# A run of extra matmuls behind the last product of a decoder trunk, into two PSUM banks that nobody reads

## The chip, the core and the metric

The kernel runs on one core of one Trainium2 chip. The metric is the device time of one execution in microseconds (us); lower is better. A difference counts as one when it is over 2%.

## The reference, cut to what matters

A small decoder trunk over 256 tokens of width 2048: a recurrent block (RG-LRU), an MLP, a dilated attention block and a second MLP, each with an RMS norm ahead of it and a residual add behind it, and a final norm.

```python
def _mlp(h, w1, w2):
    u = jnp.einsum('bsd,df->bsf', h, w1)          # 2048 -> 8192
    u = jnp.square(jax.nn.relu(u))
    return jnp.einsum('bsf,fd->bsd', u, w2)       # 8192 -> 2048

def reference(x, ...):
    for i in range(DEPTH):                        # DEPTH = 2
        h = _rmsnorm(x, mix_norm[i])
        x = x + (_rglru_block(h, ...) if i % 2 == 0 else _dilated_attention_block(h, ...))
        x = x + _mlp(_rmsnorm(x, mlp_norm[i]), mlp_w1[i], mlp_w2[i])
    return _rmsnorm(x, final_norm)
```

The change adds nothing to the result: what it computes is not in the reference.

## The kernel before

All products are made on TensorE (PE) in a rounded 32-bit float type (float32r). Each operand is split into a high part and a low part, and a product is three matmuls into the same accumulator: high by high, high by low, low by high. The still operand of a matmul (128 by 128) is loaded into the array by a weight load of its own, the moving operand is streamed through it in 128, 256 or 512 columns, and the result is added up in one of eight PSUM banks of 512 columns. Weight tiles of 128 by 2048 come by DMA into `raw`; ScalarE (ACT) makes their high part `whi`, VectorE (DVE) the low part `wlo`.

`xT` are four tiles of normed, turned activations. Each has four blocks of 512 elements, and a block holds, for 128 rows of the model's width, two token halves `t` (even and odd tokens), each as a high and a low part `u`, each of 128 tokens `q`, so its order in memory is (t u q). Where a block moves through the array it is read "in turn": one element of the even half, then one of the odd half, 256 elements apart. `moving`, `in_turn` and `by_turn` are the access patterns for this; `moving(x, 0)` is the high part of all 256 tokens, `moving(x, 1)` the low part. `mm` (line 201) issues every matmul.

The kernel opens with ten warm-up matmuls, then works through a list of items, each some 48 matmuls on one or two weight units: the recurrent block, the first MLP, attention, the second MLP. The order on PE is the order in which the Python code issues the matmuls; each engine works through its own list in order, and semaphores hold it where data or a buffer is not ready. PE is fed from the pool `psum`: `acc` (four banks), `tr` (two) and `g` (two). `g` serves the first products of the MLPs; its last use before the change is some 45 us ahead of PE's last matmul.

The last part of the program is `final_items`: the last chunk of 512 model columns is made for the first 128 tokens, normed and sent out while the second 128 tokens are computed in two banks, one half each (`first_halves`, which issues each matmul as two of 256 columns, alternating between the two banks, and `last_half`). Behind the last matmul a short chain on DVE and ACT adds the residual, forms the norm and scales the rows, and the rows go out by DMA. At the end SyncE (SP) waits for everything that is under way, and the engines meet at a barrier.

```python
    def moving(x, u):
        return x.rearrange("p (t u q) -> p u q t", t=2, u=2)[:, u]
    ...
                        mm(bank[:, s], aT(k)[:, x + 128:x + 256],
                           in_turn(w[:, j * 512:(j + 1) * 512], s.start, 256), starts, False)
```

Of the kernel before, what the change touches and what calls it, by code (L numbers as in the profile page):

```python
# [10 lines left out]
F32 = mybir.dt.float32  # L11
# [65 lines left out]
def trunk(ctx: ExitStack, tc: tile.TileContext, a: dict, out: bass.AP):  # L77
    nc = tc.nc
    P = 128
# [3 lines left out]
    psum = ctx.enter_context(tc.tile_pool(name="psum", bufs=1, space=bass.MemoryType.PSUM))  # L83
# [116 lines left out]
    def mm(o, l, r, start, stop):  # L200
        nc.tensor.matmul(o, l, r, start=start, stop=stop, skip_group_check=True)  # L201
# [6 lines left out]
    def pcol(name, j):  # L208
        at = PC[name][0] + j
        return par[:, at:at + 1]  # L210
# [3 lines left out]
    state = {}  # L214
# [5 lines left out]
    def new_xT(n):  # L220
        t = perm.tile([P, 4, 512], F32R, name=f"xT{n}")
        state["xT", n] = t
        return t
# [39 lines left out]
    def moving(x, u):  # L263
        return x.rearrange("p (t u q) -> p u q t", t=2, u=2)[:, u]
# [769 lines left out]
        state["gB"] = gB  # L1034


    first = [None] * FIRST
    lru.open("rec")
    plan_rec()
# [26 lines left out]
    for n in range(NCH):  # L1066
        x = new_xg(n)
        t = new_xT(n)
# [6 lines left out]
        for i in range(max(len(cols), len(loads))):  # L1075
# [9 lines left out]
        order = ("x0", "w0", "x1", "x2", "x3", "w1", "w2", "w3") if n == 0 else (  # L1085
            "x0", "x1", "x2", "w0", "x3", "w1", "w2", "w3")
        for what in order:
            k = int(what[1])
# [4 lines left out]
            g = pcol("mix0", 4 * n + k)  # L1093
# [39 lines left out]
    for at in range(len(items) - 1, -1, -1):  # L1133
        u = items[at][0]
        least[at] = least[at + 1] if u is None else min(u, least[at + 1])
    least = least[1:]
    for at, (u, fn, kind) in enumerate(items):
# [15 lines left out]
            sums_of_tokens()  # L1153
        now[0] += 1
    assert not later, sorted(later)
    lru.close()


# [83 lines left out]
```

## Time and profile before

| | |
|---|---|
| time, median of 2 runs | 2021.47 us (2021.29 to 2021.66) |
| the profiled execution's own time | 2022.14 us |
| its span, first to last instruction | 2020.4 us |
| mean granted TensorE clock | 0.999 |
| PE busy | 2006.2 us, 99% of the span, 13761 matmuls |
| PE weight loads | 13761 |
| DVE, ACT, POOL busy | 1724.6, 1293.7, 88.4 us |

The span leaves out 1.74 us of the execution's time, and this execution was 0.67 us above the median. In the rows below PE is the matmul engine, PEld its weight loads; a row of the timeline has the start in us, the busy time in us, the engine, the line, the operation, what it writes and reads, the shape and how many instructions are merged in it. The busy time of a matmul is from its start to the modelled end of its pipeline, so the time that a matmul takes in a stream is read from the distance of two starts.

### The profile page before, as it was taken

To read this page: it belongs to the slowest core of one execution; us is meant where nothing else is said; L and a number is where in the kernel's file an instruction comes from. 1 tells how busy PE (TensorE), PEld (TensorE's weight loads), DVE (VectorE), ACT (ScalarE), POOL (GpSimd) and SP (SyncE) were. 2 spreads that over 40 slices of the span, in tenths; PEclk is the share of its full clock that TensorE was granted. 3 is DMA by queue.
4 is the path that set the end of the run, shared out by engine and by line. 5 is a ranking of instruction groups with operands and counts; after the bars stand their busy time and mean duration, and the time that the engine had idled before them with its cause. 6 is when DMAs were issued, how large, how long until landed. Compare 5 with 4: busy or idle time off the path is not lost.

```text
span 2020.4 us, 32932 instructions
## 1 busy us (share of the span) xinstructions
PE 2006.2 (99%) x13761; PEld 1876.2 (93%) x13761; DVE 1724.6 (85%) x1903; ACT 1293.7 (64%) x1420; POOL 88.4 (4%) x83
## 2 busy tenths in 40 slices
PE   9999999999999999999999999999999999999998
PEld 9999988999999999999889989889999999999997
DVE  7999865699999999998658959857999999999985
ACT  7878775566566666665657657656666666666664
POOL 0111110000000000000000000000000000000001
PEclk9999999999999999999999999999999999999999
DMA  8555565688787788777554555456787877887774
GB/s 310 204 195 201 183 229 190 246 252 250 258 284 264 230 292 270 248 238 255 197 214 175 186 188 179 176 193 245 250 250 264 283 265 228 297 270 248 233 260 153
DMA packets 68917, 472.54 MB, mean 234 GB/s; under 512 B 7584, under 2 KB 7712, under 8 KB 13472
## 3 DMA queue, kind: packets, MB, share of 16 engines
q1 hardware_dynamic: 60416, 411.18, 54.2%
q0 software_dynamic: 8064, 58.72, 14.6%
q8 instruction: 108, 1.77, 0.3%
q10 hardware_dynamic: 288, 0.52, 0.1%
q14 instruction: 41, 0.34, 0.0%
HBM read 409.58 MB, written 2.10 MB: 204 GB/s over the span
## 4 chain that ended last, share of the span: by engine, by line
PE 91%; DVE 6%; ACT 2%; issue 1%; DMA 0%; SPq 0%; DVEq 0%; ACTq 0%
PE acc L201 44%; PE g L201 29%; PE tr L201 17%; DVE wlo L136 3%; ACT whi L132 1%; DVE qT L682 1%; PE tr L242 0%; DVE xc L686 0%; DVE c L437 0%; PE tr L853 0%; DVE sT L625 0%; DVE uu L592 0%; DVE aT L601 0%; DMA par<-in_par 0%; DVE sw L612 0%
## 5 line engine op out<-in xcount | busy, mean ns | idle before, releaser
L132 ACT ACTIVATE whi<-raw 128x2048 fp32r<-128x2048 f32 (+1 forms) x309 | 568.9, 1845 | 317.1 <-PE acc L201 163.1
L136 DVE TENSOR_TENSOR wlo<-raw,whi 128x2048 fp32r<-128x2048 f32 (+1 forms) x309 | 678.1, 2197 | 96.7 <-ACT whi L132 96.3
L201 PE MATMUL g<-xT,whi 128*128 128x256 f32 x3649 | 617.1, 275 | 0.0
L201 PEld LDWEIGHTS g<-xT,whi 128*128 128x128 f32 x3649 | 553.9, 192 | 0.0
L201 PE MATMUL g<-xT,wlo 128*128 128x256 f32 x1824 | 503.0, 276 | 0.6 <-DVE wlo L136 0.4
L201 PE MATMUL acc<-xT,whi 128*128 128x256 f32 (+1 forms) x2212 | 456.3, 301 | 0.3 <-ACT whi L132 0.3
L201 PE MATMUL acc<-xT,wlo 128*128 128x256 f32 x1360 | 374.1, 275 | 0.6 <-DVE wlo L136 0.6
L201 PEld LDWEIGHTS acc<-xT,whi 128*128 128x128 f32 x2212 | 356.3, 192 | 14.4 <-ACT whi L132 1.2
L201 PEld LDWEIGHTS g<-xT,wlo 128*128 128x128 f32 x1824 | 350.1, 192 | 2.2 <-DVE wlo L136 1.1
L201 PE MATMUL acc<-whi,aT 128*128 128x512 f32 (+1 forms) x1086 | 322.9, 374 | 0.0
L136 DVE TENSOR_TENSOR wlo<-q,whi 128x2048 fp32r<-128x2048 f32 x112 | 255.8, 2284 | 23.5 <-ACT whi L132 23.2
L132 ACT ACTIVATE whi<-q 128x2048 fp32r<-128x2048 f32 x112 | 214.4, 1915 | 79.3 <-PE g L201 53.3
L201 PEld LDWEIGHTS acc<-xT,wlo 128*128 128x128 f32 x1360 | 261.9, 193 | 1.4 <-DVE wlo L136 1.3
L201 PEld LDWEIGHTS acc<-whi,aT 128*128 128x128 f32 x1086 | 204.0, 189 | 27.6
L201 PE MATMUL tr<-whi,sT 128*128 128x512 f32 (+1 forms) x728 | 212.8, 364 | 0.9
L201 PE MATMUL acc<-wlo,aT 128*128 128x512 f32 (+1 forms) x536 | 200.8, 376 | 0.0
L132 ACT ACTIVATE whi<-qT 128x2048 fp32r<-128x2048 f32 x56 | 107.6, 1922 | 127.5 <-PE g L201 93.0
L201 PEld LDWEIGHTS tr<-whi,sT 128*128 128x128 f32 x728 | 137.7, 189 | 24.1 <-issue 6.1
L201 PE MATMUL tr<-whi,aT 128*128 128x512 f32 (+1 forms) x462 | 140.3, 373 | 0.0
L136 DVE TENSOR_TENSOR wlo<-qT,whi 128x2048 fp32r<-128x2048 f32 x56 | 127.9, 2284 | 1.3 <-ACT whi L132 1.3
L201 PE MATMUL tr<-wlo,sT 128*128 128x512 f32 x336 | 127.3, 379 | 0.0
L201 PEld LDWEIGHTS acc<-wlo,aT 128*128 128x128 f32 x536 | 101.1, 189 | 13.2
(170 smaller groups left out, 2147.5 us busy)
## 6 DMA issues: line engine op xcount, KB each, us to landing
raw<-in_w SPq DMA_DIRECT2D x172, 1024.0 KB, 6.9
q<-in_w SPq DMA_DIRECT2D x84, 1024.0 KB, 8.0
raw<-in_w_in SPq DMA_DIRECT2D x35, 1024.0 KB, 4.8
raw<-in_w_qk SPq DMA_DIRECT2D x32, 1024.0 KB, 4.8
q<-q POOLq DMA_DIRECT2D x28, 1024.0 KB, 12.2
q<-qT POOLq DMA_DIRECT2D x28, 1024.0 KB, 7.5
raw<-in_w_out SPq DMA_DIRECT2D x20, 1024.0 KB, 4.8
raw<-in_w_v SPq DMA_DIRECT2D x16, 1024.0 KB, 4.8
```

The costliest lines, as they stand in the source:

```text
L132: nc.scalar.activation(split[i][0][:, s], r, AF.Copy)
L136: nc.vector.tensor_sub(split[i][1][:, s], r, split[i][0][:, s].bitcast(F32))
L201: nc.tensor.matmul(o, l, r, start=start, stop=stop, skip_group_check=True)
L682: nc.vector.tensor_add(q[to], q[a], q[b])
```

## The change

A function `probes` is called once, behind the last item and ahead of the closing of the pools. It takes the two banks of the pool's name `g`, opens each with one matmul of 512 columns, and then issues 23 runs of 24 matmuls each that go on adding to these banks: 2 + 552 = 554 matmuls. Fifteen runs (360 matmuls) have 256 columns, eight runs (192) have 512. Nothing reads the banks. The runs differ in where the results go (one half of a bank, its two halves in turn, two banks in turn, or changing every three), in the still operand (a new block of `xT1` or `xT2` each time, each used twice, or always the same), and in the order in which the moving block of `xT0` is read.

```diff
+    def probes():
+        banks = [psum.tile([P, 512], F32, name="g", bufs=2) for _ in range(2)]
+        for b in banks:
+            mm(b, state["xT", 1][:, 0, 0:128], state["xT", 0][:, 0, :], True, True)
+        flat = [state["xT", n][:, :, :].rearrange("p k s -> p (k s)") for n in range(4)]
+        def weights(n, k):
+            return flat[1 + n][:, 128 * k:128 * k + 128]
+        def tokens(k, u):
+            return moving(state["xT", 0][:, k, :], u)
+        def run(to, still, read, count=24):
+            for j in range(count):
+                mm(to(j), weights(*still(j)), read(j), False, j == count - 1)
+        one = lambda j: banks[0][:, 0:256]
+        halves_of = lambda j: banks[0][:, 256 * (j % 2):256 * (j % 2) + 256]
+        both_of = lambda j: banks[j % 2][:, 0:256]
+        far = lambda j: banks[j % 2][:, 256 * (j % 2):256 * (j % 2) + 256]
+        thirds = lambda j: banks[0][:, 0:256] if j % 6 < 3 else banks[1][:, 0:256]
+        new = lambda j: (j % 2, j % 16)
+        real = lambda j: ((0, 0, 1)[j % 3], j // 3 % 16)
+        same = lambda j: (0, 3)
+        pair = lambda j: (0, j // 2 % 16)
+        hl = lambda j: tokens(j // 3 % 4, (0, 1, 0)[j % 3])
+        hi = lambda j: tokens(j % 4, 0)
+        fixed = lambda j: tokens(0, 0)
+        for to in (one, halves_of, both_of, far, thirds):
+            run(to, real, hl)
+        for to in (one, halves_of, both_of):
+            run(to, new, hi)
+        for to in (one, halves_of, both_of):
+            run(to, same, hi)
+        for to in (one, halves_of):
+            run(to, pair, hi)
+        run(one, new, fixed)
+        run(halves_of, same, fixed)
+        whole = lambda j: banks[0]
+        turns = lambda j: banks[j % 2]
+        for order in ("u q t", "q t u", "q u t", "u t q"):
+            run(whole, new, lambda j: state["xT", 0][:, j % 4, :].rearrange(f"p (t u q) -> p {order}", t=2, u=2))
+        run(turns, new, lambda j: state["xT", 0][:, j % 4, :].rearrange("p (t u q) -> p u q t", t=2, u=2))
+        run(whole, same, lambda j: state["xT", 0][:, j % 4, :].rearrange("p (t q) -> p q t", t=2))
+        run(whole, new, lambda j: state["xT", 0][:, j % 4, :].rearrange("p (t q) -> p q t", t=2))
+        run(turns, new, lambda j: state["xT", 0][:, j % 4, :].rearrange("p (t q) -> p q t", t=2))
...
     assert not later, sorted(later)
+    probes()
     lru.close()
```

On PE, at the end of its list, the difference begins like this (a minus stands before rows of the kernel before, a plus before rows of the changed one; `x2` merges two rows that read alike):

```order
 L201 MATMUL acc<-wlo,aT_19652 128x256
 L201 MATMUL acc<-whi,aT_19652 128x256
-L1238 UNCONDITIONAL_BRANCH
+L201 MATMUL g<-xT_13361,xT_13419 128x512 x2
+L201 MATMUL g<-xT_13361,xT_13419 128x256 x2
+L201 MATMUL g<-xT_13361,xT_13567 128x256
```

The two `acc` matmuls are the last of `last_half`, and the added ones stand directly behind them, in front of the jump that ends PE's list; all that stands ahead of them is unmoved. `xT_13361` is the moving tile `xT0`, `xT_13419` and `xT_13567` are the still tiles `xT1` and `xT2`.

On SP, the queue that ends the program, these rows stand at the end in the changed kernel, and the same rows but for the line number in the last one stand there before (the brackets name the semaphores that a row waits for):

```order
411 L977 DMA out<-xc_69 128x512 [waits Activation_49]
412 L977 DMA out<-xc_70 128x512 [waits DMAHW6_49,DVE_49]
413 L977 DMA out<-xc_68 128x512 [waits DMAHW7_49,Activation_49]
414 L977 DMA out<-xc_71 128x512 [waits DMAHW1_49,DVE_49]
415 L1288 UNCONDITIONAL_BRANCH
```

None of the stores of the result has come to wait for PE's new rows; only the closing of the program stands behind them.

## The prediction

> **What bounds the kernel now.** I read the page first: the share of each engine, the clock line and the shares of the chain that ended last.
>
> ```profile
> span 2020.4 us, 32932 instructions
> PE 2006.2 (99%) x13761; PEld 1876.2 (93%) x13761; DVE 1724.6 (85%) x1903; ACT 1293.7 (64%) x1420; POOL 88.4 (4%) x83
> PEclk9999999999999999999999999999999999999999
> PE 91%; DVE 6%; ACT 2%; issue 1%; DMA 0%; SPq 0%; DVEq 0%; ACTq 0%
> ```
>
> PE is busy for 2006.2 of 2020.4 us, it carries 91% of the chain, and its clock is full in all forty slices. It is the bound, so matmuls that are added to its list cannot be hidden beside it, except where it stands idle. The next view, the busy time by stretches (PE, PEld, DVE, ACT, POOL, then clock and DMA), tells where that is.
>
> ```profile
> 0.00:1970.00 1970.00, 1964.11 (x13544) 1838.86 (x13545) 1695.87 (x1869) 1272.70 (x1389) 79.82 (x80) 1.00 0.70 236
> 1970.00:2012.00 42.00, 42.00 (x219) 37.30 (x217) 26.16 (x26) 18.89 (x26) 8.57 (x3) 1.00 0.38 144
> 2012.00:2020.40 8.40, 0.05 (x1) 0.00 (x0) 2.60 (x9) 2.14 (x5) 0.00 (x0) 0.82 0.52 196
> ```
>
> In the last 8.40 us PE works for 0.05 us only: its last matmul ends at 2012.05. What runs there is told by the chain in order of time and by the timeline's last row, with the landing time of that store from the view of the DMAs:
>
> ```profile
> 1989.86 22.21 PE acc L201 x126
> 2014.31 1.33 ACT xc L971 x2
> 2015.67 0.38 ACTq L977 DMA_DIRECT2D out<-xc  x1
> out<-xc ACTq DMA_DIRECT2D x1, 256.0 KB, 3.2
> ```
>
> The chain goes from PE to the norm on DVE and ACT until 2015.64, the last store is issued at 2015.67 and lands 3.2 us later at 2018.9, and the other 1.5 us up to 2020.4 are the closing of the program. **This tail of 8.35 us is the only cover for the new matmuls.**
>
> **The change part by part.** Nothing is removed and nothing moved: PE's new rows stand behind its last product and wait for nothing that is not long done, since the banks of `g` were last used in the second MLP's first products. DVE, ACT and the stores do not depend on them, so the tail runs as before beside them. New are 554 matmuls, each with its weight load, and the end of the program, which must wait for PE. So the sum is: PE's end, plus 554 matmuls in a stream, plus the closing.
>
> *256 columns, 360 of them.* The chain has long pieces of such matmuls, three per block with the high weights twice and then the low ones, all into one half of one `g` bank. This is the pattern of the first new run.
>
> ```profile
> 468.54 10.72 PE g L201 x96
> 469.94 0.30 PEld L201 LDWEIGHTS g<-xT,whi 128*128 128x128 f32 x2
> ```
>
> 10.72 us for 96 is 0.1117 us each. The second row shows that the still operand is loaded anew even where it is the same as that of the matmul before (two loads of `whi` in succession; all in all 13761 loads for 13761 matmuls). So the runs with a kept still operand are priced like those with a new one. The runs that alternate are also in the trace, in `first_halves`, where each matmul goes to the other bank and the other half than the one before:
>
> ```profile
> 2007.42 0.39 PE L201 MATMUL acc<-wlo,aT 128*128 128x256 f32 x2
> 2008.09 0.39 PE L201 MATMUL acc<-wlo,aT 128*128 128x256 f32 x2
> 2008.76 0.39 PE L201 MATMUL acc<-wlo,aT 128*128 128x256 f32 x2
> ```
>
> Between the first and the last of these rows lie twelve matmuls (two rounds of six) in 1.34 us, again 0.1117 us each. Where the result goes has no price here. Why 0.1117 and not less is told by attention, where five matmuls on `qk` have 256 columns in four of them and 128 in one:
>
> ```profile
> 1121.17 0.72 PE L201 MATMUL g<-qk 128*128 128x256 f32 x5
> 1121.73 0.38 PE L201 MATMUL acc<-xT,whi 128*128 128x512 f32 x1
> ```
>
> The five take 0.56 us, 0.112 each, although one of them streams half as much. The stream runs at the pace of the weight loads, one in 0.112 us, whatever is streamed up to 256 columns. That leaves nothing for the alternation to win, and 360 x 0.1117 = 40.2 us. If without this pace a matmul of 256 columns took half of one of 512 (0.108, next row), the sum would be 1.3 us less; that is the lower bound for kept operands that need no load.
>
> *512 columns, 194 of them with the two that open the banks.* In the last products of the second MLP:
>
> ```profile
> 1995.09 0.38 PE L201 MATMUL acc<-wlo,aT 128*128 128x512 f32 x1
> 2004.81 0.38 PE L201 MATMUL acc<-wlo,aT 128*128 128x512 f32 x1
> ```
>
> The first and the last of sixteen such rows stand 15 rounds of three apart: 9.72 / 45 = 0.216 us each. 194 x 0.216 = 41.9 us.
>
> *The order of reading.* Of the eight runs of 512 columns, five read as the kernel does now, two elements 256 apart in turn. The orders "q t u" and "q u t" go round four places, 128 elements apart; no row has four places, but `in_turn` with 64, 128 and 256 elements between its two places occurs in attention and the MLPs, and the rows above show one pace for them. I price these two orders at 0.216 as well. The order "u t q" reads 128 neighbours in a row, and so do the two opening matmuls, 512 in a row: 26 matmuls without a row of their own. The lower end is 0.216, the pace at all distances that there are. The upper end comes from the only matmuls that read 32-bit neighbours, the transposes of the norm (another type, and in transpose mode):
>
> ```profile
> 303.03 1.04 PE L242 MATMUL tr<-con,xc 128*128 128x128 f32 x8
> 303.82 0.46 PE L201 MATMUL acc<-whi,aT 128*128 128x512 f32 x1
> 304.12 0.38 PE L201 MATMUL acc<-wlo,aT 128*128 128x512 f32 x1
> ```
>
> From 303.03 to 304.12 there are eight transposes and one matmul of 512 columns: (1.09 - 0.216) / 8 = 0.109 us for 128 columns, 0.436 for 512, twice the pace of the others. Below 0.216 nothing in the trace goes. I take 0.216, since the type and the mode of the 512-column rows are those of the new runs, and keep 26 x (0.436 - 0.216) = 5.7 us as the price of the other end.
>
> [...]
>
> *The closing.* SP's last waits now end with PE instead of with the last store. Of the 1.5 us of closing, some part can be done while PE still works; I take 1.0 us and keep 0 and 1.5 as bounds.
>
> *The sum.* New matmuls 40.2 + 41.9 = 82.1 us. PE ends at 2012.05 + 82.1 = 2094.15, long after the last store at 2018.9, so the tail (8.35 us) is wholly hidden and of the 82.1 us some 74 to 75 are seen. Span 2094.15 + 1.0 = 2095.15; with the 1.74 us outside the span, 2096.9 against the profiled execution's 2022.14. The median of the runs lies 0.67 us under that execution, so the forecast is **2096.2 us, 3.7% slower**. 2% (2061.9 us) is about what a measurement of this kernel can tell from no change.
>
> **The rivals.**
>
> A, the forecast: one pace per width, 2096.2 us, whatever bank, half, operand or order.
>
> B: neighbours in memory are read at half the pace. For it stand the transposes; against it that they are of another type and mode, and that the pace of the other rows does not depend on the distance. Time 2096.2 + 5.7 = 2101.9 us. A wider form has the two four-place orders slow as well: 74 matmuls x 0.22 = 16.3 us, 2112.5 us; the equal pace at three distances speaks against it.
>
> C, not slower: matmuls that write to a bank which no one waits for overlap. The trace has a hint, the row at 303.82: it starts 0.03 us after the last transpose (303.03 + 7 x 0.109 = 303.79). If the new ones followed each other like that, 554 x 0.03 = 16.6 us, half of it under the tail, and the end would be 2096.2 - 82.1 + 16.6 = 2030.7 us, within 2%. It decides from the point where 554 take less than 47.8 us (2061.9 - 2096.2 + 82.1), under 0.086 us each. Against it: the matmul behind that row comes 0.30 later, so the early start is paid back at once, and `first_halves` alternates banks and halves at 0.1117.
> [...]
>
> D: the new matmuls are not run at all, as nothing reads them: 2021.5 us. Against it, they stand one by one in PE's built list.
>
> **How the numbers follow.** A 0.62; B 0.25, its wider form 0.07; C 0.02, of it half within 2% and half still slower; D 0.015; the remaining 0.025 for other kinds (a lower clock in the last stretch, and 0.005 for a gain that nothing here shows). The range reaches from A with the 1.3 us for kept operands and 0.6 of the closing taken off, 2094.3, to B with the closing at its 1.5, 2102.4; A and B inside are 0.87. What is left out, the wider form of B, C, D and the rest, is 0.13. Faster by over 2% has 0.005, within 2% (D and half of C) with 0.025, slower by over 2% with 0.97.
>
> **What would show it.** In the profile after, PE's rows up to the last `acc` matmul and the stretch 0 to 2012 should be as before. Behind it should stand 15 runs of 24 at 2.68 us each and eight at 5.18, with no gap between them, a weight load for every matmul, and clock 1.00. Case B shows as one run of 24 that takes some 10 us and two opening matmuls that take 0.9 together. Runs with kept operands or with halves in turn that take under 2.6 us would show the pace of the loads wrong. The norm's rows on DVE and ACT and the last store should stand at the same times as before, beside the new rows; if the stores came late, the tail would not be independent, as I took it to be. The distance from PE's end to the end of the span shows the closing. The forecast is wrong by more than its range if the pace of the loads does not hold without fresh data behind it, or if an order with four places is slow.

## The result and the profile after

The changed kernel takes 2100.41 us (2099.84 to 2100.98, two runs) against 2021.47 us before: a ratio of 1.039 (95% interval 1.0346 to 1.0435). The forecast was 2096.2 us with a range of 2094.3 to 2102.4. The direction held and the time lies inside the range. The mechanism held too, but for one term, the price of the order in which the moving block is read; the sum was 4.2 us too small.

The page of the profile after has 554 matmuls more on PE, as many loads more, and a full clock to the end:

```profile
span 2099.2 us, 34040 instructions
PE 2090.8 (100%) x14315; PEld 1951.5 (93%) x14315; DVE 1722.9 (82%) x1903; ACT 1294.2 (62%) x1420; POOL 88.6 (4%) x83
PEclk9999999999999999999999999999999999999999
PE 90%; DVE 6%; ACT 1%; issue 1%; DMA 1%; SPq 0%; DVEq 0%; ACTq 0%
```

The stretches (PE, PEld, DVE, ACT, POOL, clock, DMA) are those of before up to 2012, but for 0.6 us by which this execution was later. Behind it PE, which was idle there before, works without a pause, and DVE and ACT do the 2.6 and some 2 us of work of the old tail:

```profile
0.00:1970.00 1970.00, 1962.55 (x13541) 1836.83 (x13542) 1693.87 (x1868) 1272.56 (x1388) 79.97 (x80) 1.00 0.70 236
1970.00:2012.00 42.00, 42.00 (x217) 37.38 (x216) 26.47 (x26) 19.15 (x27) 8.61 (x3) 1.00 0.38 145
2012.00:2058.00 46.00, 46.00 (x391) 45.32 (x391) 2.60 (x9) 2.45 (x7) 0.00 (x0) 1.00 0.12 42
```

The chain in order of time now ends with the new rows, and the timeline has the last store where it was, 0.6 us later with everything else:

```profile
1999.95 12.70 PE acc L201 x82
2012.65 85.60 PE g L201 x554
2016.27 0.38 ACTq L977 DMA_DIRECT2D out<-xc  x1
```

So the new rows take 85.6 us where the sum had 82.1, and PE ends at 2098.25. From there to the end of the span are 0.95 us, the closing, which I had at 1.0.

Where the 3.5 us lie is read by counting PE's matmuls in stretches of 4.40 us (or 2.00) inside single runs: time, PE busy (matmuls), clock, DMA.

```profile
2016.00:2018.00 2.00, 2.00 (x21) 1.00 0.92 343
2034.60:2036.60 2.00, 2.00 (x20) 1.00 0.03 8
2053.40:2057.80 4.40, 4.40 (x22) 1.00 0.00 0
2059.00:2063.40 4.40, 4.40 (x17) 1.00 0.00 0
2066.00:2070.40 4.40, 4.40 (x17) 1.00 0.00 0
2072.50:2076.90 4.40, 4.40 (x21) 1.00 0.02 4
2093.00:2097.40 4.40, 4.40 (x22) 1.00 0.00 0
```

A count is one or two too high at 512 columns and two or three at 256, since matmuls that are under way when the stretch begins count too; so it tells 0.283 from 0.216, and 0.227 only with the starts. The first two rows are runs of 256 columns (halves in turn, and always the same still operand). Then come the orders "u q t", "q t u", "q u t", "u t q" and the last run. The two four-place orders have 17 matmuls where the others have 21 or 22. From the starts of all matmuls in the trace, the mean distance in each run is:

```
runs                                        columns   us per matmul   forecast
15 runs: one, halves, banks, far, thirds;       256     0.1117         0.1117
  still operand new, in pairs, the same
"u q t" into one bank                           512     0.216          0.216
"q t u" (four places)                           512     0.283          0.216
"q u t" (four places)                           512     0.283          0.216
"u t q" (runs of 128 neighbours)                512     0.227          0.216 (other end 0.436)
two opening matmuls (512 neighbours)            512     0.236          0.216 (other end 0.436)
last four runs, in turn                         512     0.216          0.216
```

48 x 0.067 = 3.2 us for the four-place orders and 24 x 0.011 + 2 x 0.02 = 0.3 us for the neighbours make up the 3.5.

### The profile page after: what moved, and what is told of

It reads as the page before. It is cut to its first block, busy times and chain, and to the rows that moved or that the text cites. A ratio compares the mean times of both kernels' runs of the same rounds, so it can differ in the third digit from the quotient of the medians.

```text
span 2099.2 us, 34040 instructions
## 1 busy us (share of the span) xinstructions
PE 2090.8 (100%) x14315; PEld 1951.5 (93%) x14315; DVE 1722.9 (82%) x1903; ACT 1294.2 (62%) x1420; POOL 88.6 (4%) x83
## 3 DMA queue, kind: packets, MB, share of 16 engines
q1 hardware_dynamic: 60416, 411.18, 52.5%
## 4 chain that ended last, share of the span: by engine, by line
PE 90%; DVE 6%; ACT 1%; issue 1%; DMA 1%; SPq 0%; DVEq 0%; ACTq 0%
PE acc L201 41%; PE g L201 32%; PE tr L201 16%; DVE wlo L136 3%; ACT whi L132 1%; DVE qT L682 1%; DMA raw<-in_w_in 0%; PE tr L242 0%; DVE c L437 0%; DVE xc L686 0%; DMA xg<-in_xT 0%; PE tr L853 0%; DVE sT L625 0%; DVE uu L592 0%; DVE aT L601 0%
```

## The experiments

My theories after the result: the pace of the loads explains 0.1117, and the order of reading explains what the sum lacked. The rival to the first is a fixed surcharge on narrow matmuls; the rival to the second is time lost at the start of the new rows or in the closing. In what follows "us per matmul" is the distance of two starts. The edits are shown in short form, and what stands behind `#` in them is not in the kernels.

**Undoing the orders.** The three orders that came out slow are read as "u q t":

```diff
-        for order in ("u q t", "q t u", "q u t", "u t q"):
+        for order in ("u q t", "u q t", "u q t", "u q t"):
```

> The changed kernel with the orders q t u, q u t and u t q read as u q t instead; all else as in the change. Theory (the order of reading is what the sum had too small): these three runs fall from 6.79, 6.80 and 5.45 us to 5.18 each, 3.5 us less, 2096.9 us. Rival (the time was lost elsewhere, at the start of the new rows or in the closing): 2100.4 us as in the change.

Measured: 2096.59 us (2096.42 to 2096.79), ratio 1.037 (1.0352 to 1.0387). The same three runs, counted as above:

```profile
2057.80:2062.20 4.40, 4.40 (x22) 1.00 0.00 0
2063.00:2067.40 4.40, 4.40 (x22) 1.00 0.00 0
2068.20:2072.60 4.40, 4.40 (x22) 1.00 0.00 0
```

All three have 22, at 0.216 each. With them at the forecast pace the kernel takes what was forecast to within 0.4 us. The rival is out: at the start and in the closing no more than that can have been lost. The three orders were undone together, so what each of them cost is read from its own starts, in the table above.

**The pace of the loads, first try.** New runs of 64 to 512 columns in place of the old ones:

```diff
+        for n in (64, 128, 192, 256, 288, 320, 384, 448, 512):
+            run(lambda j: banks[0][:, 0:n], new, lambda j: places(j, 2, n))     # two places in turn
+        for n in (256, 320, 384, 448, 512):
+            run(lambda j: banks[0][:, 0:n], new, lambda j: block(j)[:, 0:n])    # neighbours
+        for n in (256, 320, 384, 448, 512):
+            run(lambda j: banks[0][:, 0:n], new, lambda j: places(j, 4, n))     # four places
```

> Other new rows: 24 matmuls each of 64, 128, 192, 256, 288, 320, 384, 448, 512 columns read two places in turn, then 256 to 512 columns read as neighbours, then 256 to 512 read four places in turn. Load-pace theory: 0.112 us for all two-place widths up to 256, then 0.123 at 288, 0.136 at 320, 0.162 at 384, 0.216 at 512; rival (a fixed surcharge on narrow matmuls): 0.030 at 64, 0.058 at 128. On the order of reading, theory stream (a price per column): four places 0.143 at 256, 0.178 at 320, 0.213 at 384, 0.248 at 448, 0.283 at 512, neighbours 0.143 at 320, 0.171 at 384. Rival load (the price is a collision with the weight load below, one sum per matmul): four places 0.203 at 320, 0.230 at 384, 0.257 at 448, neighbours 0.147 at 320, 0.174 at 384.

Measured, two places: 0.112 at 64 columns, 0.123 at 288, 0.136 at 320, 0.162 at 384, 0.189 at 448, 0.216 at 512. The rival's 0.030 at 64 columns is out. But the runs of 128 and 192 columns and the start of the one of 256 read 0.21, which no theory had. The stretches tell why: the granted clock fell to a half.

```profile
2016.50:2019.50 3.00, 3.00 (x16) 0.50 0.89 335
2021.00:2025.00 4.00, 4.00 (x21) 0.50 0.00 0
2028.80:2031.40 2.60, 2.60 (x24) 1.00 0.00 0
```

By the trace's record of the clock it was at a half from 2016.38 to 2026.62, 10.24 us, beginning some 3.3 us after the start of the run of 64 columns, while PE's busy row reads 100%. In the changed kernel 360 matmuls of 256 columns at the same 0.112 us each kept clock 1.00, so between the two it is not the pace that differs but the columns streamed, 64 against 256. What the clock goes by, no run here tells. So this run could not settle the widths of 128 and 192.

On the order with four places it did: from 320 columns on it took 0.176, 0.213, 0.247 (448) and 0.283 (512), within 1% of the theory of a price per column (0.178, 0.213, 0.248) and 4 to 13% below a fixed sum per load (0.203, 0.230, 0.257). At 256 it took 0.137, 4% below the 0.143 of the price per column. On neighbours it did not. They took 0.120 at 256 columns, then 0.147, 0.175, 0.206 and 0.229. At 320 and 384 that is what the fixed sum had said (0.147, 0.174) and not the price per column (0.143, 0.171); at 448 neither fits, since two places took 0.189 there and the fixed sum adds 0.011. What the price of neighbours goes by stays open.

**The pace of the loads, second try.** To keep the clock up, narrow matmuls alternate with ones of 512 columns (the clock of this run reads 1.000 on the mean); then the still operand gets narrower:

```diff
+        for n in (32, 64, 128, 192, 256):
+            w = lambda j: n if j % 2 == 0 else 512
+            run(lambda j: banks[0][:, 0:w(j)], new, lambda j: places(j, 2, w(j)))
+        thin(64, 128); thin(64, 64); thin(32, 64)      # (still columns, moving columns in turn with 512)
+        thin_all(64, 256); thin_all(32, 256); thin_all(128, 256)
```

> Other new rows, 24 matmuls per run, all with a new still operand: first matmuls of 32, 64, 128, 192 and 256 columns in turn with one of 512, so that the array stays busy and its clock full; then the same with 64 and 32 instead of 128 columns of the still operand (128 and 64 moving columns in turn with 512 by 64 still ones, 64 in turn with 512 by 32 still ones), and 256 moving columns throughout by 64, 32 and 128 still ones. Theory (the load of the next still operand sets a least time of 0.112 us that falls with the still operand's columns): every pair with 128 still columns takes 0.216 + 0.112 = 0.327 us, from 32 to 256 moving columns; with 64 still columns the pairs take 0.275 (128) and 0.272 (64), with 32 about 0.245, and 256 columns throughout by 64 or 32 take 0.109, by 128 0.112. Rival (narrow matmuls have a fixed surcharge of 0.003 to 0.005, whatever the load): 0.232, 0.246, 0.275, 0.301 and 0.327 for the five pairs, and 0.112 with fewer still columns too.

Stretches of 3.30 us in the pairs with 32 and with 256 columns and in the first pair with 64 still columns, then 2.80 us with 32 still ones (matmuls under way at the start of a stretch count too, up to three here, so the counts show that the first two pairs are alike, and the starts by how much):

```profile
2012.50:2015.80 3.30, 3.30 (x23) 1.00 0.37 132
2028.30:2031.60 3.30, 3.30 (x23) 1.00 0.00 0
2032.10:2035.40 3.30, 3.30 (x27) 1.00 0.00 0
2038.70:2041.50 2.80, 2.80 (x25) 1.00 0.00 0
```

By the starts, all five pairs with 128 still columns take 0.3275 us, from 32 to 256 moving columns. With 64 still columns both pairs take 0.2742, with 32 the pair takes 0.2476. Taking off the 0.2158 of the 512-column one leaves 0.1117, 0.0584 and 0.0318 us for a load of 128, 64 and 32 columns: 0.833 ns per still column and 5 ns. And 256 moving columns throughout take 0.1092 with 64 or 32 still columns, 0.1117 with 128. This is the theory, within about 1% in every row, and the fixed surcharge (0.232 for the pair with 32 columns) is out. In these rows a matmul takes the longer of its stream and the next load, and 256 columns by 128 are 2.5 ns on the load's side (0.1117 against 0.1092).

The same run has early starts like the one in rival C: in the pair of 32 and 512 columns the starts lie 0.028 and 0.299 apart, 0.327 together as in the other pairs. An early start does not mean that the pair became shorter.

**How places are read.** All 512 columns, in other orders:

```diff
+        for d in (2, 4, 8, 16, 32, 64, 128):
+            run(whole, new, lambda j: near(j, 2, d))      # two places, d elements apart
+        for d in (4, 16, 32, 64):
+            run(whole, new, lambda j: near(j, 4, d))      # four places
+        run(whole, new, lambda j: near(j, 8, 64))
+        run(whole, new, lambda j: near(j, 16, 32))
+        for s in (2, 3, 4):                               # one place, every s-th element
+            run(whole, new, lambda j: flat[0][:, 0:512 * s].rearrange("p (q s) -> p q s", s=s)[:, :, 0])
```

> Other new rows, all of 512 columns: two places in turn at a distance of 2, 4, 8, 16, 32, 64, 128 elements, four places at 4, 16, 32, 64, eight at 64, sixteen at 32, then one place with a step of 2, 3, 4. Theory lines (two short lines are held open, and each new line beyond that costs): two places 0.216 at any distance of a line or more, distance 2 like neighbours (0.227), four places 0.283 at every distance, eight and sixteen no better, step 2 some 0.24, step 4 0.283. Rival banks (what counts is whether reads that follow each other hit the same bank, by the distance): the distances differ, some two-place distances as slow as 0.28 and some four-place ones as fast as 0.216.

Counts in 4.40 us: two places at 2, at 4 and at 128; four at 4 and at 32; eight; sixteen; a step of 2, of 4.

```profile
2012.50:2016.90 4.40, 4.40 (x21) 1.00 0.55 205
2018.00:2022.40 4.40, 4.40 (x22) 1.00 0.03 11
2044.00:2048.40 4.40, 4.40 (x22) 1.00 0.00 0
2049.00:2053.40 4.40, 4.40 (x18) 1.00 0.00 0
2062.00:2066.40 4.40, 4.40 (x18) 1.00 0.00 0
2075.50:2079.90 4.40, 4.40 (x11) 1.00 0.00 0
2087.00:2091.40 4.40, 4.40 (x11) 1.00 0.00 0
2098.00:2102.40 4.40, 4.40 (x11) 1.00 0.00 0
2119.00:2123.40 4.40, 4.40 (x11) 1.00 0.00 0
```

Two places take 0.216 at every distance from 4 elements (16 bytes) on and 0.228 at 2; four take 0.268 to 0.283; eight 0.488, sixteen 0.434; a step of 2, 3 or 4 takes 0.451, 0.450 and 0.460. The theory of lines held for two places, and for four roughly (0.268 at the small distances, 0.273 at 32 elements and 0.283 at 64, where it had 0.283 at each; why the distance counts there is open). It failed for the steps: step 2 should have been 0.24 and step 4 0.283, and both take 0.45 to 0.46. The lines themselves were an assumption of mine, which no run shows. The rival of banks is out for two places: from 16 bytes to 1 KB the distance makes no difference (0.216).

**Runs of neighbours.** Two, four or more neighbours at each place:

```diff
+        for e in (2, 4, 8, 32):                           # two places, e neighbours at each
+            run(whole, new, lambda j: block(j).rearrange("p (b q e) -> p q b e", b=2, e=e))
+        ...                                               # four places, e = 2
+        ...                                               # 2 of every 4; 4 of every 8; 4 of every 16
+        ...                                               # two places, step 2; two places, step 4
+        run(whole, new, lambda j: flat[0][:, 2 + 512 * (j % 3):514 + 512 * (j % 3)])
```

> Other new rows, all of 512 columns: two places in turn with runs of 2, 4, 8, 32 neighbours at each; four places with runs of 2; then one place: 2 neighbours of every 4, 4 of every 8, 4 of every 16; two places each with a step of 2, and of 4; neighbours from an odd pair on. Theory pairs (memory is read in pairs of 8 bytes, one pair in 0.88 ns = 0.450/512, and two places can be under way at once): runs of 2 at two places 0.216 to 0.227, four places with runs of 2 0.227 or less, 2 of every 4 and 4 of every 8 0.227, two places with a step 0.45 or, if the two places overlap, 0.22. Rival lines (16 bytes are read at once, and it needs four hits): 2 of every 4 as slow as step 2, 0.450; 4 of every 8 or 16 0.227.

Measured: two places with 2 neighbours at each 0.339, with 4, 8 and 32 0.250, 0.243 and 0.237; four places with 2 each 0.446; 2 of every 4 0.452; 4 of every 8 0.232 and of every 16 0.231; two places with a step of 2 0.227, of 4 0.452; neighbours from an odd pair on 0.234. In stretches of 4.40 us (2 at two places; 2 of every 4; 4 of every 8; two places with step 2, with step 4):

```profile
2014.00:2018.40 4.40, 4.40 (x15) 1.00 0.54 203
2050.00:2054.40 4.40, 4.40 (x11) 1.00 0.00 0
2061.00:2065.40 4.40, 4.40 (x21) 1.00 0.00 0
2072.00:2076.40 4.40, 4.40 (x21) 1.00 0.01 4
2078.00:2082.40 4.40, 4.40 (x11) 1.00 0.00 0
```

The theory of pairs is out (2 of every 4 should have been 0.227). That of lines has 2 of every 4 and 4 of every 8 right and fails elsewhere: by it two places with a step of 2 should be as slow as one place with that step, and they run at 0.227 against 0.451. No rule that I tried fits all rows. What is shown is the table, not its cause.

**Still operands and types.** Four places and neighbours with one still operand throughout, with one read at a step of 2, with one that is shifted; then bf16 operands, made from a block by one copy on ACT.

```diff
+        run(whole, same, lambda j: places(j, 4))
+        run(whole, same, lambda j: block(j))
+        run_by(whole, step_w, lambda j: places(j, 4))     # every second element as still operand
+        ...
+        run_by(whole, wb, lambda j: t)                    # t, wb: bf16
+        run_by(whole, wb, lambda j: t.rearrange("p (b q) -> p q b", b=2))
+        run_by(half, wb, lambda j: t[:, 0:256])
```

> Other new rows: four places and neighbours with a still operand that is always the same (also with the same moving block), then with a still operand read at a step of 2 elements (four places, neighbours, two places, and two places of 256 columns), four places with a still operand shifted by 4 to 12 elements, four plain runs, then bf16 operands of 512 columns as neighbours, two and four places, and of 256 as neighbours and two places. Theory stream: 0.283 and 0.227 whatever the still operand. Rival load: other numbers with the stepped or shifted operand. Load-pace theory: the stepped operand of 256 columns 0.112 or, if the load gets slower, more; bf16 at 256 columns 0.109, as its load is shorter. If the price of the order is one of bytes: bf16 neighbours 0.216, four places at most 0.283.

Four places took 0.283 and neighbours 0.227 with a kept still operand, as with a new one; with the stepped one 0.273 and 0.234, and with the shifted one 0.278. So the price of four places, 0.067 us, is for the most part one of the moving side; the still operand shifts these times by 4% at most. For neighbours, whose whole price is 0.011, the 0.006 that the stepped operand adds is half of it. 256 columns at two places went from 0.112 to 0.120 with the stepped operand. In bf16 the order counts the other way round: neighbours take 0.216 and two places 0.484, both at full clock (22 and 10 in 4.40 us). The run of four places, at 0.865, fell for the most part into a stretch of half clock (0.54 on the mean from 2097.3 to 2116), which came after 12 us of two places, so it tells nothing of the order. 256 columns of bf16 as neighbours take 0.109 once the clock is back, 2.5 ns less than the 32-bit ones, as the theory of the loads has it for a shorter load (bf16 loads were busy for 0.098 us each, 32-bit ones for 0.189); at two places they take 0.243.

```profile
2080.00:2084.40 4.40, 4.40 (x22) 1.00 0.00 0
2086.00:2090.40 4.40, 4.40 (x10) 1.00 0.00 0
2119.20:2120.70 1.50, 1.50 (x16) 1.00 0.00 0
```

**What the order is worth in the kernel itself.** No new rows; the moving blocks of the kernel before are read as neighbours, and the tokens and columns of the result are not put back into their order:

```diff
-        return x.rearrange("p (t u q) -> p u q t", t=2, u=2)[:, u]                  # moving
+        return x.rearrange("p (t u q) -> p u t q", t=2, u=2)[:, u]
-        return w.rearrange("p (t q) -> p q t", t=2)[:, at // 2:(at + n) // 2, :]    # in_turn
+        return w[:, at:at + n]
         ...                                                                         # products of queries and keys
```

> The kernel before, without new rows, where in_turn, moving and the products of queries and keys read their moving blocks as neighbours instead of two places in turn (the score and value products of attention keep theirs). The columns come out in another order, so the order of tokens and columns in the result is left out. Counted from the groups by shape: 4374 matmuls of 512 columns and 9055 of 256. Theory (the price of neighbours holds in the whole kernel, as measured in the run of widths: 0.120 for 256 columns against 0.112, 0.228 for 512 against 0.216): 9055 x 0.0084 + 4374 x 0.0125 = 131 us more, 2150 us. Rival (256 columns stay at 0.115, as a pure rate per column would have it): 2098 us. Rival (the price belongs to rows that have the memory to themselves, and is hidden or drowned beside DVE and ACT): 2021 to 2030 us.

Measured: 2089.14 us (2089.03 to 2089.38), ratio 1.0333 (1.0319 to 1.0347), 67.2 us more. The groups by shape have the same counts as before and longer busy times. Before, then with neighbours:

```profile
L201 PE MATMUL g<-xT,whi 128*128 128x256 f32 x3647 | 616.9, 275 | 0.0
L201 PE MATMUL acc<-whi,aT 128*128 128x512 f32 x1026 | 312.4, 380 | 0.0
```

```profile
L201 PE MATMUL g<-xT,whi 128*128 128x256 f32 x3647 | 627.3, 277 | 0.0
L201 PE MATMUL acc<-whi,aT 128*128 128x512 f32 x1026 | 323.5, 390 | 0.0
```

By the starts, 512 columns took 0.2285 on the mean (before 0.2162) and 256 columns 0.1143 (before 0.1120): 4374 x 0.0123 + 9055 x 0.0023 = 75 us, of which 67 are seen. Summed over all starts of the two traces, waits included, the distances grow by 47.9 us at 512 columns and 19.4 us at 256, 67.3 in all: the other 8 us are waits of the kernel before that the slower stream took up. So the price of neighbours at 512 columns holds in the kernel, beside DVE and ACT and DMAs. At 256 columns it does not: the 0.120 of the first try on the pace was read as 256 in a row, here most are two rows of 128. Whether that is the reason was not tested. The expectation of 2150 us carried that 0.120 over and was 61 us too high; the pure rate per column, 2098, was nearer.

**Using the pace: halves of a bank added later.** Three matmuls of 256 columns cost 0.335, one of 512 and one of 256 cost 0.327. The first products of the MLPs can be issued so, if the two halves of the bank are added afterwards. The new matmuls stand in a function of their own, which is called in place of the old one:

```diff
-            mm(ps[:, at:at + cut], hi[:, s], xh[...], ...); mm(ps, hi[:, s], xl, ...); mm(ps, lo[:, s], xh, ...)
+            mm(ps, hi[:, s], x.rearrange("p (t u q) -> p u q t", t=2, u=2), ...)
+            mm(ps[:, :S], lo[:, s], moving(x, 0), ...)
...
+        nc.scalar.activation(uu, ps[:, S:], AF.Copy)
+        nc.vector.tensor_add(uu, uu, ps[:, :S])
```

> The kernel before, without new rows, where the first products of both MLPs issue high weights against high and low tokens as one matmul of 512 columns into both halves of the bank (as attention's queries and keys do), and ACT and DVE add the halves before the squared ReLU. Theory (loads pace the 256-column matmuls at 0.112, so three of them take 0.335 and 512 + 256 take 0.216 + 0.112 = 0.327): 128 units x 16 x 7.7 ns = 15.8 us less, 2005.7 us. Rival (the two operations more per unit on ACT and DVE, some 0.8 us each, hold up the weight splitting): 2021 us or more.

> As the run before, but the sum of the halves on DVE is issued one item later, so that DVE does not wait for the copy on ACT. Theory: 2005.7 us. If the wait of DVE for ACT is what costs in the run before, this one is nearer to 2005.7 than that; if the work itself costs, both are alike.

Measured: 2098.08 us (2096.38 to 2099.98, ratio 1.0377, 1.0363 to 1.0391) and, with the sum one item later, 2074.43 us (2071.76 to 2076.45, ratio 1.0262, 1.0248 to 1.0276). The matmuls do take what was forecast (the later form shows 0.218 and 0.109 in turn), but PE now waits for DVE. What PE waited for, first in the kernel before, then in the later form (total us, times, longest):

```profile
PE acc L201 <- DVE wlo L136: 1.6, 3, 0.6
PE g L201 <- DVE wlo L136: 0.4, 2, 0.2
```

```profile
PE acc L201 <- DVE sT L640: 26.1, 14, 3.5
PE g L201 <- DVE uu L606: 18.9, 12, 1.6
PE tr L201 <- DVE xc L701: 9.9, 14, 0.7
```

How much room DVE had is told by 90 us of the first MLP, before the change and in the later form (PE, PEld, DVE, ACT, POOL, clock, DMA):

```profile
470.00:560.00 90.00, 89.94 (x648) 85.08 (x648) 85.44 (x81) 57.40 (x50) 3.42 (x4) 1.00 0.83 277
```

```profile
470.00:560.00 90.00, 85.96 (x468) 76.27 (x467) 84.03 (x86) 57.02 (x56) 3.68 (x5) 1.00 0.79 246
```

Before the change DVE is busy for 85.44 of 90 us there, 95%, not the 85% of the page: 4.56 us were free. In the later form nine sums, 3.72 us, stand in this stretch. By that measure they would have fitted with 0.8 us left for all waits. Issuing the sum one item later took back 24 of the 76 us that were lost, so the wait of DVE for the copy on ACT, 85.6 us in 79 waits in the first form, was a part of the loss. What the rest is was argued, not shown. The 128 sums take some 53 us of DVE in all, and the later form is 52.5 us above the kernel before, which fits the work itself; but DVE is busy for 93% of the stretch there, not for all of it, and waits for ACT for 6.1 us of it (3.0 before), so the place of the sums in the order can have a part in it. No version here beats the kernel before.

## Why the prediction was right, and where it was off

- **PE is the bound and the tail the only cover**: held. The new rows stand on the chain for 85.6 us, the stores and the norm ran beside them unmoved. The profiled span grew by 78.8 us: 85.6 of new rows, less the 8.35 of the old tail, and with it 0.95 of closing and 0.6 by which the part ahead of the change ended later.
- **256 columns at 0.1117 whatever bank, half or operand**: held in all fifteen runs, to 0.0003 us. The reason I gave, the pace of the loads, was argued from one row; the second try on the pace, with its pairs of narrow and wide matmuls, shows it: 0.1117, 0.0584 and 0.0318 us for a load of 128, 64 and 32 columns.
- **A kept still operand is loaded anew**: held. 554 more matmuls came with 554 more loads.
- **512 columns at 0.216**: held in five of the eight runs, "u q t" and the last four, and in the three others as soon as their order was undone.
- **The order of reading**: this is the mis-sized term, and A in its own words (one pace per width, whatever the order) did not hold. I priced "q t u" and "q u t" like two places, by a pace that does not depend on the distance. The rows that I had could not show that: before the change all in-turn rows of 512 columns have 256 elements between their places, and those with 64 or 128 have at most 256 columns and go at the pace of the loads. The independence is real (0.216 from 16 bytes to 1 KB, by the later run), but it says nothing on the number of places: four take 0.283, 3.2 us in all. My bound, 16.3 us for the three orders from the transposes, 10.6 of it for these two, was above it; I gave it 0.07 and left it outside the range. I had also named a slow order with four places as a sign that the range would break. It was slow, and the range held because the price was under a third of what I had for it.
- **Neighbours**: I took 0.216 and kept 0.436 as the other end. They take 0.227, 0.3 us in all, near the lower end; the transposes are no model for them. Two places 1 KB apart, at 0.216, are cheaper than neighbours by 5%. What does take about twice as long are eight places (0.488) and single places with a step of 2 (0.451) or 4 (0.460).
- **The closing**: 0.95 us, taken at 1.0. Of the 4.2 us, 0.6 came from the part ahead of the change, which ended that much later in the execution that was profiled, and 0.1 from how that execution stands to the median.
- **Rival C** is out: alternating banks changed nothing (0.1117 either way), and the early start is paid back (0.028 and 0.299 in one pair). **D** is out: all 554 are in the profile.

So the range held by luck: it was drawn to the other end of one unknown (5.7 us for neighbours), while 3.2 of the 3.5 us came from another that I had set to nothing.

## What to carry to other kernels

Price a matmul in a stream as the longer of its moving columns and the load of the next still operand, both read from the distance of starts (here 0.1117 us by the load at 256 columns, 0.216 by the stream at 512), and expect nothing from the bank or half it writes to (0.1117 in each of the five choices here). A measured independence (of the distance of two places) covers only what it was measured on; a pattern with no row needs a bound inside the range. And ahead of shortening PE by work on another engine, read that engine's share in the stage itself: 95% there was hidden in 85% on the page.

## What the runs showed of the hardware that was not expected

- In these runs TensorE's 32-bit moving operand streamed fastest when read at two places in turn, 16 bytes or more apart (0.216 us for 512 columns). Neighbours cost 5 to 6% more (0.227 to 0.229), four places 24 to 31% (0.268 to 0.283), eight and sixteen places and single steps of 2 to 4 some 100% or more (0.434 to 0.488). In bf16 neighbours took 0.216 and two places 0.484.
- A run of 24 matmuls of 64 columns, one per 0.112 us, was followed by a clock of a half, from some 3.3 us after its start and for 10.24 us, with PE at 100% busy by the profile. At half clock matmuls of 128 and 192 columns alike took 0.213 us, where the load's pace at full clock is 0.112: 1.9 times as long.
- In the second try on the pace the load of a 32-bit still operand took 0.833 ns per column and 5 ns (0.0318, 0.0584 and 0.1117 us at 32, 64 and 128 columns).
